# A hybrid attention and mLSTM layer whose input projection is computed by Strassen's seven products

## The chip, the cores and the metric

The kernel runs on one core of a Trainium2 chip. The metric is the device time of one execution in microseconds (us), the median of several runs, lower being better. All arrays are in float32. A float32 product on TensorE is made here from three matmuls in a faster format: each operand is split into a high part (`hi`, the rounded value) and a low part (`lo`, what the rounding left out), and hi·hi, hi·lo and lo·hi are added in PSUM.

## The reference

The layer takes 2048 tokens of width 1024, norms and modulates them, projects them to 4608 columns and 16 gate columns, and sends these into a neighbourhood attention (8 heads of 64, 8 x 16 windows on a grid of 32 x 64 tokens) and a bidirectional mLSTM (4 heads of 128). Both results are gated, joined and projected back to 1024 columns.

```python
h = rmsnorm(h_res, norm_w[l]) * (1.0 + scale[:, None, :]) + shift[:, None, :]
...
proj = h @ w_in + b_in
(na_q, na_k, na_v, na_z, ml_q, ml_k, ml_v, ml_o, ml_z, i_f, f_f, i_b, f_b) = jnp.split(proj, split_idx, axis=-1)
na_out = neighbourhood_attention(na_q, na_k, na_v, rpb) * jax.nn.silu(na_z)
qk = jax.nn.silu(centred_short_conv(jnp.concatenate([ml_q, ml_k], axis=-1), conv_w, conv_b))
...
h_fwd = mlstm_chunkwise(mq, mk, mv, i_f, f_f)
h_bwd = flip(mlstm_chunkwise(flip(mq), flip(mk), flip(mv), flip(i_b), flip(f_b)))
hm = (h_fwd + h_bwd) ... * jax.nn.sigmoid(ml_o)
...
return jnp.concatenate([na_out, ml_out], axis=-1) @ w_out
```

The mLSTM carries, for each head and direction, a 128 x 128 state and a 128-vector through the sequence in chunks (of 128 tokens in this kernel), and each chunk's output needs the state before it. Its queries and keys pass through a convolution over five neighbouring tokens first.

## The kernel before

The tokens lie in SBUF, transposed, as four groups of 512 (`hhi`, `hlo`: 128 partitions x 8 k-tiles x 512). The 4608 columns are 18 blocks of 256; a block's weights are loaded by the SP queue (`load_w`), copied to `hi` by ScalarE (L199, L907) and subtracted to `lo` by GpSimd (L200, L908). The program is one stream per engine, each run in order; a scheduler has fixed that order, and a wait on one instruction holds back all that stands behind it on its engine.

- Start, about 0 to 120 us: modulation vectors on VectorE (L236), row scales, transposes on TensorE (L265), the split into `hi` and `lo` (L270 to L272), and the first two column blocks (L310).
- Token blocks, to about 360 us (`tok_blocks`): six blocks with tokens stationary and 256 columns moving (`mm3`, L513 to L515), results in token rows, evicted by a VectorE addition of the bias (L548, L568), and stored to DRAM. Beside them run the gates' scans and the decay tables (`decays`): GpSimd adds a mask to 128 x 1024 values (L779, 16 times), ScalarE takes eight exponentials of each (L783), and the result goes to the DRAM tile `d_ck`, which holds per head and chunk all that the mLSTM reads.
- Convolution blocks, to about 550 us (`conv_blocks`): four blocks with weights stationary and 512 tokens moving; ScalarE evicts them (L842), VectorE runs the five taps (one L875, four L877), and the queue stores them.
- mLSTM, to about 1005 us (`phase1b`): per head a first pass (`ml_pass1`) that carries the states of both directions over 15 steps and keeps all of them, and a second pass (`ml_pass2`) over 16 chunks that reads a chunk (`ck`), forms scores (L1142), their products (L1155, L1157), the normalised output (L1162 to L1178) and its gate (GpSimd L1179). The last eight blocks' matmuls (`nq_gen`, L934, 512 tokens in the order of the attention's patches) are fed in between by `pump`: 180 ahead, 5.5 a step of pass one and 13 a chunk of pass two.
- Phase 2, to the end: attention over 16 patches, the output projection (L1488) and the last norm. What `pump` has left, up to 108 matmuls, runs in its first slots.

## Time and profile before

| | |
|---|---|
| median of 3 runs | 1398.98 us (1396.51 to 1407.89) |
| the profiled execution's own time | 1400.58 us |
| its span, from first to last instruction | 1398.8 us |
| mean granted TensorE clock | 0.983 |
| TensorE (PE) busy | 1308.0 us, 94% |
| VectorE (DVE) busy | 819.5 us, 59% |
| ScalarE (ACT) busy | 550.2 us, 39% |
| GpSimd (POOL) busy | 261.9 us, 19% |
| moved by DMA | 265.23 MB, mean 190 GB/s |

Busy time counts an instruction from its start to its modelled end, so matmuls that overlap in the pipeline show long durations (0.28 to 0.40 us) although one starts every 0.12 to 0.23 us; the time that a series of them takes is read from start to start. Rows of the profile name a line of the kernel, the engine, the operation, the tile written and the tiles read, shapes, the count, the busy time and the mean in ns, and then how long the engine sat idle before and what ended that idleness.

### The profile page before, as it was taken

What the parts mean: (1) busy time and instruction counts of PE and PEld (TensorE: products, weight loads), DVE (VectorE), ACT (ScalarE), POOL (GpSimd) and SP (SyncE); (2) the same over time, 40 slices, a digit from 0 to 9 for tenths busy, and PEclk for the clock granted to TensorE, in tenths of its full rate; (3) what the DMA queues carried; (4) which work ended last, traced back from release to release, by engine and by line L of the source; (5) the groups of instructions that cost most, each with busy time, mean ns of one, the idle gap of its engine ahead of it and who ended that gap; (6) DMA issues with size and microseconds to landing.
All of it is one profiled execution on the core that took longest, in us unless ns stands there. A gap on an engine that the chain in (4) does not pass through costs nothing. (4 is left out here: it accounts for less than half of the span.)

```text
span 1398.8 us, 23244 instructions
## 1 busy us (share of the span) xinstructions
PE 1308.0 (94%) x8026; PEld 1119.5 (80%) x8026; DVE 819.5 (59%) x2585; ACT 550.2 (39%) x1160; POOL 261.9 (19%) x281
## 2 busy tenths in 40 slices
...
GB/s 370 237 301 159 120 170 228 175 173 195 99 90 216 176 200 161 148 170 158 201 201 218 238 204 249 211 132 174 167 251 227 185 228 169 197 192 170 191 159 75
DMA packets 270090, 265.23 MB, mean 190 GB/s; under 512 B 32746, under 2 KB 232714, under 8 KB 269974
## 3 DMA queue, kind: packets, MB, share of 16 engines
...
## 5 line engine op out<-in xcount | busy, mean ns | idle before, releaser
L934 PE MATMUL pq<-hlo,whi_a 128*128 128x512 f32 x512 | 210.1, 410 | 0.0
L934 PE MATMUL pq<-hhi,whi_a 128*128 128x512 f32 x512 | 210.0, 410 | 0.0
L934 PE MATMUL pq<-hhi,wlo_a 128*128 128x512 f32 x512 | 209.7, 410 | 0.0
L1415 ACT ACTIVATE pbuf<-pbuf,mn 128x480 f32<-128x480 f32 (+5 forms) x128 | 76.4, 597 | 120.9 <-DVE mn L1414 107.3
L934 PEld LDWEIGHTS pq<-hhi,whi_a 128*128 128x128 f32 x512 | 97.4, 190 | 18.0
L934 PEld LDWEIGHTS pq<-hhi,wlo_a 128*128 128x128 f32 x512 | 97.2, 190 | 18.1
L934 PEld LDWEIGHTS pq<-hlo,whi_a 128*128 128x128 f32 x512 | 97.4, 190 | 17.8
L1488 PE MATMUL y<-hhi,whi_a 128*128 128x512 f32 x256 | 84.8, 400 | 0.4 <-ACT whi_a L1461 0.4
L1488 PE MATMUL y<-hhi,wlo_a 128*128 128x512 f32 x256 | 84.4, 399 | 0.0
L1414 DVE CUSTOM_DVE_ANT_0 pbuf<-pS,tab 128x480 f32<-128x480 f32 (+5 forms) x128 | 65.3, 540 | 31.7 <-PE pS L1409 15.6
L908 POOL TENSOR_TENSOR wlo_a<-rawq,whi_a 128x1024 fp32r<-128x1024 f32 x20 | 48.4, 2419 | 162.5 <-ACT whi_a L907 123.8
L1179 POOL TENSOR_TENSOR hm<-hm,ck 128x128 f32<-128x128 f32 x64 | 26.4, 413 | 265.7 <-DVE hm L1178 219.9
L1160 ACT ACTIVATE num<-px,gtile 128x129 f32<-128x129 f32 x120 | 38.4, 365 | 96.1 <-PE px L1155 76.7
L1087 DVE TENSOR_SCALAR wv<-kv,gtile 128x129 f32<-128x129 f32 x120 | 37.0, 315 | 62.8 <-PE dc L1103 35.2
L783 ACT ACTIVATE dec<-dec,gtile 128x128 f32<-128x128 f32 x128 | 41.5, 391 | 79.1 <-POOL dec L779 76.4
L1451 PE MATMUL pO<-pt,v 128*64 128x128 f32 (+3 forms) x832 | 61.8, 283 | 9.9 <-ACT pt L1438 9.4
L548 DVE TENSOR_TENSOR stv<-pv,brow 128x256 f32<-128x256 f32 x32 | 12.2, 419 | 95.4 <-DMA d_vna<-stv 59.1
L1451 PEld LDWEIGHTS pO<-pt,v 128*64 128x64 f32 (+3 forms) x832 | 45.5, 137 | 26.6 <-issue 11.9
L1436 PE MATMUL pT<-ident,pbuf 128*128 128x128 f32 (+2 forms) x416 | 59.8, 283 | 1.7 <-DVE pbuf L1426 1.7
L1438 ACT ACTIVATE pt<-pT 96x384 f32<-96x384 f32 (+3 forms) x128 | 57.7, 500 | 0.7 <-PE pT L1436 0.7
L779 POOL TENSOR_TENSOR dec<-dec,mask 128x1024 f32<-128x1024 f32 x16 | 38.1, 2381 | 94.2 <-DMA dec<-d_mneg 78.2
L1488 PEld LDWEIGHTS y<-hhi,whi_a 128*128 128x128 f32 x256 | 47.2, 188 | 10.0 <-ACT whi_a L1461 0.6
...
## 6 DMA issues: line engine op xcount, KB each, us to landing
...
kv<-d_ck SPq DMA_DIRECT2D x120, 128.5 KB
...
```

What stands on the lines that cost most here:

```text
L779: nc.gpsimd.tensor_tensor(t, t, mask.unsqueeze(2).broadcast_to([P, 2, 4, CH]), ALU.add)
L783: nc.scalar.activation(t[:, d, o, :], t[:, d, o, :], AF.Exp, bias=self.cols["g"][:, d, h, c : c + 1])
L908: nc.gpsimd.tensor_tensor(lo[:, :, cs], raw, hi[:, :, cs].bitcast(F32), ALU.subtract)
L934: nc.tensor.matmul(patch_ps(ps) if patch else ps, w, self.htok(h, g, k, patch), start=(k == 0 and n == 0), stop=(k == KT - 1 and n == 2))
L1087: nc.vector.tensor_scalar(wv, tiles[d, i][:, 128:257], self.cols["w"][:, d, h, c : c + 1], None, ALU.mult)
L1160: nc.scalar.activation(num[:, d, :], px[:, d, :], AF.Copy, scale=self.cols["inter"][:, d, h, c : c + 1])
L1414: nc.vector.tensor_tensor_reduce(pt[:, :nk], ps, tabs[place[u]][j][:, :nk], 1.0, 3e38, ALU.add, ALU.min, mn)
L1415: nc.scalar.activation(pt[:, :nk], pt[:, :nk], AF.Exp, bias=mn, scale=-1.0, accum_out=sums[:, j : j + 1])
L1436: nc.tensor.transpose(ps[:cs, i, :], pts[j][:, i * cs : (i + 1) * cs], self.ident)
L1438: nc.scalar.activation(t[:cs, :nch, :], ps[:cs, :nch, :], AF.Copy)
L1451: nc.tensor.matmul(po[j * HD : (j + 1) * HD, :], v[:n, h * HD : (h + 1) * HD], pt[j][:n, i, :], start=(i == 0), stop=(i == nch - 1))
L1488: nc.tensor.matmul(y, m[:, k, :], w[k][:, cs], start=(k == 4 and n == 0), stop=(k == 3 and n == 2))
```

## The change

The input projection is a product of a 2048 x 1024 token matrix with a 1024 x 256 weight matrix, 18 times. Tokens are taken in two pairs of groups, (2, 3) first and (0, 1) after it. Within a pair the token matrix is cut into four quarters (two groups by two halves of the 1024), and the weights too (two halves of the 1024 by two of the 256 columns), and seven products of quarters or sums of quarters, with further sums, take the place of eight. `stream` runs them: every product is 12 matmuls of 128 x 512 (four k-tiles, three each), with weights stationary, so 2 x 18 x 7 x 12 = 3024 matmuls in all.

- Token operands: `first` and `second` transpose the tokens, form four sums on VectorE (`sums`) and split eight quarters into `hi` and `lo` (`halved`, on GpSimd and VectorE).
- Weight operands: seven per block, four of them sums (`make_sums`, VectorE), each split by ScalarE and GpSimd (`rounded`; one of seven by VectorE) into a ring of eight tiles. The upper stream makes them and stores each one (0.5 MB) to the DRAM tile `d_w`; the lower stream loads them again (`provide`).
- Results: three copies (ScalarE) and four additions (VectorE) per block put the seven products together (`result`). All blocks now come out with channels on partitions; the six that are wanted in token rows are transposed (`turned`). The patch order is made by the eviction's access pattern. Gate columns are computed apart (`gate_rows`).
- The convolution runs over a pair of groups; the two tokens on the border are repaired at the end (`fix_border`). The zero edges are set by GpSimd instead of VectorE.
- The decays run in the lower stream: GpSimd adds the mask and the gate column (two operations on 128 x 1024 values per group), ScalarE takes one exponential; the loads for it are issued by GpSimd.
- The table fills, the output weights' scaling and the tables' rows run in the upper stream.
- mLSTM: pass one carries the backward state only, with its weighting on GpSimd; pass two carries the forward state along (`forward`), reads whole `d_ck` rows, and the first scaling of its output is on ScalarE. Twelve blocks of the lower stream are fed in between by `pump`: 60 ahead, 3.5 a step and 12 a chunk. All of them are drained before phase 2.
- Phase 2 loads all keys from DRAM at its start; half of them lay in SBUF before.

```diff
-PUMP0 = 180
-PUMP1 = 5.5
-PUMP2 = 13
-PUMP3 = 5
+NB = 18
+UPPER, LOWER = (2, 3), (0, 1)
+DENSE = 6
+PUMP0 = 60
+PUMP1 = 3.5
+PUMP2 = 12
...
-    def mm3(self, ps, lhi, llo, rhi, rlo):
-        nc = self.nc
-        for k in range(KT):
-            nc.tensor.matmul(ps, lhi(k), rhi(k), start=(k == 0), stop=False)
-            nc.tensor.matmul(ps, lhi(k), rlo(k), start=False, stop=False)
-            nc.tensor.matmul(ps, llo(k), rhi(k), start=False, stop=(k == KT - 1))
...
-    def ch_tile(self, ps, slot, sub, g, patch=False):
-        hi, lo = slot
-        self.mm3(
-            ps,
-            lambda k: hi[:, k, sub * P : (sub + 1) * P],
-            lambda k: lo[:, k, sub * P : (sub + 1) * P],
-            lambda k: self.htok(self.hhi, g, k, patch),
-            lambda k: self.htok(self.hlo, g, k, patch),
-        )
...
+        upper = self.stream(0, UPPER, self.upper_hook)
+        self.first(upper)
...
+        lower = self.stream(NB, LOWER, lambda n: None)
+        self.second(lower)
...
+        self.chain = itertools.chain(self.gate_chain(cp, self.gates), self.decays(cp))
+        for at in lower:
+            if at == (DENSE - 1, "p3", 11):
+                break
...
+    def sums(self, f11, f12, f21, f22):
+        nc = self.nc
+        nc.vector.tensor_add(f22, f21, f22)
+        nc.vector.tensor_sub(f21, f11, f21)
+        nc.vector.tensor_sub(f11, f22, f11)
+        nc.vector.tensor_sub(f12, f12, f11)
...
+    def gate_rows(self, pair):
+        nc = self.nc
+        for gi, terms in enumerate(((("a11", 0), ("a12", KH)), (("s1", 0), ("a22", KT)))):
+            ps = self.turn_tile(f"pg_{pair[gi]}")[0:32]
+            for j, (nm, k0) in enumerate(terms):
+                for k in range(KH):
+                    for n, h in enumerate(self.op[nm, k]):
...
+    def rounded(self, q, i, src, eng=None):
+        nc = self.nc
+        t = self.wpart(q, i)
+        nc.scalar.activation(t[:, 0], src, AF.Copy)
+        (eng or nc.gpsimd).tensor_tensor(t[:, 1], src, t[:, 0].bitcast(F32), ALU.subtract)
+        dst = self.d_w[ORDER_UPPER[q], i]
+        store = lambda: nc.sync.dma_start(dst, t.bitcast(F32).rearrange("p h k c -> p (h k c)"))
+        if q < 2:
+            store()
+        else:
...
+    def make_sums(self, q, which=(2, 3, 4, 5)):
+        nc = self.nc
+        b11, b12, b21, b22 = self.quarters(q)
+        if 2 in which:
+            self.t2[q] = t2 = self.sp.tile([P, GT], F32, tag="sp", name=f"t2_{q}").rearrange("p (a b) -> p a b", a=KH)
+            nc.vector.tensor_sub(b11, b12, b11)
+            nc.vector.tensor_sub(t2, b22, b11)
+            nc.vector.tensor_sub(b21, b21, t2)
+            nc.vector.tensor_sub(b12, b22, b12)
+        for i in which:
+            if i == 2:
+                self.rounded(q, i, self.t2.pop(q), nc.vector)
+            else:
+                self.rounded(q, i, {3: b12, 4: b11, 5: b21}[i])
...
+    def provide(self, q, i):
+        if q < NB:
+            if i == 5:
+                self.make_sums(q)
+            elif i in (0, 1, 6):
+                self.make(q, i)
+        elif q < 2 * NB:
+            t = self.wpart(q, i)
+            self.nc.sync.dma_start(t.bitcast(F32).rearrange("p h k c -> p (h k c)"), self.d_w[ORDER_LOWER[q - NB], i])
...
+    PRODUCTS = {
+        "p1": ("x", "a11", "b11", True),
+        "p2": ("w", "a12", "b21", True),
+        "p6": ("x", "s2", "t2", False),
+        "p7": ("y", "s3", "t3", True),
+        "p5": ("x", "s1", "t1", False),
+        "p4": ("v", "a22", "t4", True),
+        "p3": ("x", "s4", "b22", False),
+    }
...
+        for n in range(2, NB):
+            plan += [(n, "p1"), (n - 1, "p4"), (n - 1, "p3"), (n, "p2"), (n, "p6"), (n, "p7"), (n, "p5")]
+        plan += [(NB - 1, "p4"), (NB - 1, "p3")]
+        for n, pn in plan:
+            q, blk = q0 + n, order[n]
...
+            w = self.wpart(q, i)
+            for k in range(KH):
+                hi, lo = self.op[a, k]
+                for m, (wh, h) in enumerate(((0, hi), (0, lo), (1, hi))):
+                    nc.tensor.matmul(ps, w[:, wh, k], h, start=(first and k == 0 and m == 0), stop=(k == KH - 1 and m == 2), skip_group_check=True)
+                    if k < KH - 1 or m < 2:
+                        yield n, pn, 3 * k + m
+            self.result(q, blk, pn, pair)
+            self.provide(*divmod(7 * q + i + 8, 7))
+            self.boundary()
+            yield n, pn, 11
...
+        if pn == "p1":
+            copied(1, 0)
+        elif pn == "p2":
+            placed(0, 0, w, c.pop((q, 1)))
+        elif pn == "p6":
+            copied(2, 0)
+        elif pn == "p7":
+            nc.vector.tensor_add(c[q, 2], y, c[q, 2])
+        elif pn == "p5":
+            copied(3, 1)
+            placed(1, 1, y, c.pop((q, 3)))
+        elif pn == "p4":
+            placed(0, 1, v, c.pop((q, 2)))
+        else:
...
+    def turned(self, blk, s, g, f):
+        ps = self.turn_tile(f"tt_{blk}_{s}_{g}")
+        for j in range(4):
+            nc.tensor.transpose(ps[:, j * P : (j + 1) * P], f[:, j * P : (j + 1) * P], self.ident)
...
+        nc.vector.tensor_copy(a[:, GT + 2 : GT + 4], b[:, 2:4])
+        nc.vector.tensor_copy(b[:, 0:2], a[:, GT : GT + 2])
+        nc.gpsimd.memset(a[:, 0:2], 0.0)
+        if g0 == UPPER[0]:
+            nc.gpsimd.memset(b[:, GT + 2 : GT + 4], 0.0)
...
             nc.gpsimd.tensor_tensor(t, t, mask.unsqueeze(2).broadcast_to([P, 2, 4, CH]), ALU.add)
-            for d in range(2):
-                for o in range(4):
-                    c = 4 * gi + o
-                    nc.scalar.activation(t[:, d, o, :], t[:, d, o, :], AF.Exp, bias=self.cols["g"][:, d, h, c : c + 1])
+            nc.gpsimd.tensor_tensor(t, t, self.cols["g"][:, :, h, cs].unsqueeze(3).broadcast_to([P, 2, 4, CH]), ALU.add)
...
+            nc.scalar.activation(t, t, AF.Exp)
...
-        self.st = [[None] * NC for _ in range(2)]
+        self.st = [None] * NC
...
         def weight(i):
-            for d in range(2):
-                c = i if d == 0 else NC - 1 - i
-                wv = ml.tile([P, 129], F32, tag=f"wv{d}", bufs=2, name=f"wv_{h}_{d}_{i}")
-                nc.vector.tensor_scalar(wv, tiles[d, i][:, 128:257], self.cols["w"][:, d, h, c : c + 1], None, ALU.mult)
-                wvs[d, i] = wv
+            c = NC - 1 - i
+            wvs[i] = ml.tile([P, 129], F32, tag="wv1", bufs=2, name=f"wv_{h}_1_{c}")
+            nc.gpsimd.tensor_scalar(wvs[i], tiles[i][:, 128:257], self.cols["w"][:, 1, h, c : c + 1], None, ALU.mult)
...
+        def weight(c):
+            wvs[c] = ml.tile([P, 129], F32, tag="wv0", bufs=2, name=f"wv_{h}_0_{c}")
+            nc.gpsimd.tensor_scalar(wvs[c], vo[c][0], self.cols["w"][:, 0, h, c : c + 1], None, ALU.mult)
+        def forward(c):
+            dc = self.ms.tile([P, GT], F32, tag="s1", bufs=3, name=f"dc_{h}_0_{c}")[:, :129]
+            nc.tensor.matmul(dc, kt.pop(c), wvs.pop(c), start=True, stop=True)
+            new = ml.tile([P, 129], F32, tag="stf", bufs=2, name=f"stf_{h}_{c}")
+            if c == 0:
+                nc.vector.tensor_copy(new, dc)
+            else:
+                nc.vector.scalar_tensor_tensor(new, fw[c], self.decay[:, h, c : c + 1], dc, ALU.mult, ALU.add)
+            fw[c + 1] = new
...
-            nc.vector.tensor_scalar(t, num[:, 0, 0:128], r[:, 0:1], None, ALU.mult)
+            nc.scalar.activation(t, num[:, 0, 0:128], AF.Copy, scale=r[:, 0:1])
...
+        def keys(ct, cols):
...
+        for ct in range(NH // 2):
+            keys(ct, slice(T // 2, T))
```

Two places of the order of instructions, first GpSimd's while it works on the decay tables. Before, it stands in the token blocks; `stvo` is the staging tile of a token block's results, `wlo` the low part of a weight block, `dec` a decay table.

```order
L779 TENSOR_TENSOR dec_1_2232<-dec_1_2232,mask 128x1024
L560 MEMSET stvo_0_2164 128x4
L200 TENSOR_TENSOR wlo_a<-raw_0_2155,whi_a 128x4x256
L200 TENSOR_TENSOR wlo_a<-raw_1_2159,whi_a 128x4x256
L560 MEMSET stvo_1_2306 128x4
L779 TENSOR_TENSOR dec_2_2334<-dec_2_2334,mask 128x1024
```

Now it stands in the lower stream; `u` is the input tile of the convolution, and L696 sets its edge.

```order
L962 DMA dec_3_4717<-d_mneg 128x512 x2
L971 TENSOR_TENSOR dec_2_4692<-dec_2_4692,mask 128x1024
L696 MEMSET u_1_0_4802 128x2
L696 MEMSET u_0_0_4845 128x2
L972 TENSOR_TENSOR dec_2_4692<-dec_2_4692,gtile 128x1024
L962 DMA dec_0_4741<-d_mneg 128x512 x2
L971 TENSOR_TENSOR dec_3_4717<-dec_3_4717,mask 128x1024
L972 TENSOR_TENSOR dec_3_4717<-dec_3_4717,gtile 128x1024
```

A table takes two operations and two DMA issues of GpSimd instead of one operation, and the small MEMSETs that open a convolution tile are queued among them.

The second place is VectorE in the convolution blocks. Before, the taps follow one another with edge copies and MEMSETs of VectorE's own, and no eviction stands among them.

```order
L847 COPY u_0_1_3871<-u_0_2_3909 128x2
L846 COPY u_0_3_3948<-u_0_2_3909 128x2
L875 TENSOR_SCALAR acc_k_2_3962<-u_0_2_3909,cw 128x512
L877 SCALAR_TENSOR_TENSOR acc_k_1_3914<-u_0_1_3871,cw,acc_k_1_3914 128x512
L877 SCALAR_TENSOR_TENSOR acc_k_2_3962<-u_0_2_3909,cw,acc_k_2_3962 128x512
```

Now, in the lower stream, evictions stand behind taps; `py` and `pv` are PSUM banks, `c` a partial sum, `hal` the kept border tokens.

```order
L714 TENSOR_SCALAR acc_0_5008<-u_0_0_4845,cw 128x512
L716 SCALAR_TENSOR_TENSOR acc_1_4817<-u_1_1_4712,cw,acc_1_4817 128x512
L716 SCALAR_TENSOR_TENSOR acc_0_5008<-u_0_0_4845,cw,acc_0_5008 128x512 x2
L605 TENSOR_TENSOR c_21_4884<-py_4911,c_21_4884 128x512
L595 TENSOR_TENSOR u_1_1_4950<-py_4911,c_21_4948 128x512
L695 COPY u_0_1_5000<-u_0_0_4845 128x2
L701 COPY u_0_1_5000<-hal 128x2
L702 COPY hal<-u_1_1_4950 128x2
L595 TENSOR_TENSOR u_0_1_5000<-pv_4987,c_21_4884 128x512
```

The additions L605 and L595, which free TensorE's banks, are queued behind the first tap (L714) of `u_0_0_4845`, whose edge is set by GpSimd's MEMSET of the piece above.

1216 lines of the change are left out of this document (569 added, 647 removed).

## The prediction

> **What bounds the kernel now.** I read the page's busy times first, then the busy time by stage, then the timeline of TensorE inside each stage, and last what it waited for.
>
> ```profile
> PE 1308.0 (94%) x8026; PEld 1119.5 (80%) x8026; DVE 819.5 (59%) x2585; ACT 550.2 (39%) x1160; POOL 261.9 (19%) x281
> ```
>
> ```profile
> 0.00:60.00 60.00, 33.30 (x199) 30.72 (x200) 42.06 (x79) 29.02 (x45) 35.49 (x33) 0.94 0.80 303
> 60.00:360.00 300.00, 280.36 (x2261) 274.38 (x2261) 83.41 (x229) 139.41 (x253) 64.03 (x44) 0.97 0.72 190
> 360.00:557.00 197.00, 192.70 (x860) 154.91 (x859) 125.53 (x238) 58.78 (x87) 20.84 (x8) 1.00 0.63 160
> 557.00:1005.00 448.00, 432.12 (x2299) 360.33 (x2298) 307.25 (x1193) 132.06 (x276) 70.69 (x85) 1.00 0.66 189
> 1005.00:1399.00 394.00, 369.48 (x2415) 299.13 (x2413) 261.21 (x847) 190.90 (x500) 70.87 (x112) 0.97 0.77 188
> ```
>
> A row gives the stretch, its length, the busy time of TensorE, its weight loads, VectorE, ScalarE and GpSimd, the granted clock, the DMA share and GB/s. TensorE is the bound of every stage after the first 60 us. No other engine is above 70% there, and VectorE is at 64% (125.53 of 197) in the convolution stage.
>
> What TensorE's work costs is the distance from one start to the next:
>
> ```profile
> 271.78 0.28 PE L514 MATMUL pv<-wlo_a,hhi 128*128 128x256 f32 x1
> ...
> 273.91 0.28 PE L514 MATMUL pv<-wlo_a,hhi 128*128 128x256 f32 x1
> ```
>
> ```profile
> 504.63 0.40 PE L514 MATMUL pc<-hlo,whi_a 128*128 128x512 f32 x1
> ...
> 507.87 0.40 PE L513 MATMUL pc<-hhi,whi_b 128*128 128x512 f32 x1
> ```
>
> ```profile
> 739.67 0.39 PE L934 MATMUL pq<-hhi,wlo_a 128*128 128x512 f32 x1
> 739.90 0.40 PE L934 MATMUL pq<-hhi,whi_a 128*128 128x512 f32 x1
> 740.14 0.39 PE L934 MATMUL pq<-hlo,whi_a 128*128 128x512 f32 x1
> 740.37 0.40 PE L934 MATMUL pq<-hhi,wlo_a 128*128 128x512 f32 x1
> ```
>
> The first pair spans 18 starts, 0.118 us each at 256 columns; the second 14, 0.231 us at 512; the last rows 0.233 us at 512 in patch order. Patch order costs nothing worth naming, and a 512-wide matmul costs no more per column than two of 256.
>
> **The projection's matmuls.** Before: 2304 of 256 columns (six blocks), 768 of 512 (convolution), 1536 in patch order. 2304 x 0.118 + 768 x 0.231 + 1536 x 0.233 = 272 + 177 + 358 = 807 us. After: 3024 x 0.231 = 699 us. **Minus 108 us**, all on the engine that bounds.
>
> **What TensorE gets in addition.** Six blocks come out channel-major and are turned back: 48 tiles of four transposes. Four transposes take 0.35 us before the next matmul starts:
>
> ```profile
> 47.44 0.60 PE L265 MATMUL tp<-ident,x 128*128 128x128 f32 x4
> 47.79 0.37 PE L310 MATMUL pvo<-whi_a,hhi 128*128 128x272 f32 x1
> ```
>
> 48 x 0.35 = 17 us. The gate columns are 64 matmuls of 512, 15 us. **Plus 32 us.**
>
> **The start.** Up to 360 us the matmuls of the six blocks (272) and 32 groups of transposes (11) leave 77 us unused. They go to the first 60 us and to stalls such as this one:
>
> ```profile
> DVE stv L548 <- DMA d_vna<-stv: 59.1, 5, 20.4
> ```
>
> ```profile
> 346.11 0.58 PE L513 MATMUL pv<-whi_b,hhi 128*128 128x256 f32 x1 [10.12 <-DVE stv L548]
> 346.49 0.42 PE L514 MATMUL pv<-wlo_b,hhi 128*128 128x256 f32 x1
> 346.71 0.41 PE L515 MATMUL pv<-whi_b,hlo 128*128 128x256 f32 x1
> ...
> 351.61 0.33 PE L514 MATMUL pv<-wlo_b,hhi 128*128 128x256 f32 x1
> 351.78 0.28 PE L515 MATMUL pv<-whi_b,hlo 128*128 128x256 f32 x1
> ```
>
> VectorE waited 20.4 us for a staging tile whose store had not landed, TensorE 10.12 us for VectorE, although the DMA engines were at 0.6 to 0.7. Behind it the matmuls start 0.21 us apart, near twice 0.118.
>
> The new start is a chain of VectorE and GpSimd. These rows carry it:
>
> ```profile
> L236 DVE CUSTOM_DVE_ANT_0 junk<-wmod,crow 128x1024 f32<-128x1024 f32 x16 | 26.9, 1682 | 0.3
> L272 DVE TENSOR_TENSOR hlo<-h,hhi 128x512 fp32r<-128x512 f32 x24 | 16.6, 691 | 39.2 <-ACT hhi L271 39.2
> L908 POOL TENSOR_TENSOR wlo_a<-rawq,whi_a 128x1024 fp32r<-128x1024 f32 x20 | 48.4, 2419 | 162.5 <-ACT whi_a L907 123.8
> ```
>
> Modulation is the same bytes in half pieces, 27 us; 32 operations for the token sums and their low parts and ten for the weight sums are 42 x 0.69 = 29 us; GpSimd's 19 low parts at half of 2.42 us are 23 us. Done one after another, which the rows on the taps below ask for, with some 6 us of small operations that is 85 us, in which TensorE has only 60 matmuls and 32 groups of transposes, 25 us. So 60 us are lost where 77 were: **minus 17 us**. If the two engines overlap fully it is 23 us less. `second` has eight low parts on GpSimd ahead of its first product: **plus 10 us** (0 if it runs under the last blocks of the upper stream).
>
> **mLSTM.** A chunk of pass two is now:
>
> ```profile
> 740.60 0.61 PE L1155 MATMUL px<-st,ck 128*128 128x129 f32 x4
> 741.05 0.61 PE L1157 MATMUL pi<-ck 128*128 128x129 f32 x4
> ...
> 744.74 0.61 PE L1155 MATMUL px<-st,ck 128*128 128x129 f32 x4
> ```
>
> ```profile
> L1113 DVE SCALAR_TENSOR_TENSOR st<-st,gtile,dc 128x129 f32<-128x129 f32 x112 | 35.8, 345 | 0.5 <-PE dc L1103 0.3
> ```
>
> That is 4.14 us, filled with projection matmuls. One state product moves from a step of pass one into the chunk, one fill goes: about 4.1 us as before. VectorE gains the state update (0.345 us, L1113) and loses a scaling to ScalarE; GpSimd's weighting replaces VectorE's. TensorE stays in front, so I price this part at nothing beyond the products already counted. The cover is TensorE's own fill; without it a chunk costs VectorE's chain.
>
> **The boundary.** The 108 matmuls that filled phase 2's first slots (25 us) are among the 108 us saved, but a slot without fill waits for its own softmax, and the first keys (4 MB, at the 408 GB/s below 10 us) come after everything is drained. **Plus 10 us**, between 0 (loads run under the last chunk) and 25.
>
> TensorE alone then gives 1400.6 - 108 + 32 - 17 + 10 + 10 = 1328 us. The profiled execution is 1.6 us over the median, so **1326 us** for the median.
>
> **What VectorE and GpSimd take from each other.**
>
> ```profile
> 429.24 0.74 DVE L877 SCALAR_TENSOR_TENSOR acc_k<-u,cw,acc_k 128x512 f32<-128x512 f32 x1
> ...
> 429.90 0.48 DVE L875 TENSOR_SCALAR acc_k<-u,cw 128x512 f32<-128x512 f32 x1
> 430.29 3.54 DVE L877 SCALAR_TENSOR_TENSOR acc_k<-u,cw,acc_k 128x512 f32<-128x512 f32 x2
> 430.86 5.26 POOL L200 TENSOR_TENSOR wlo_a<-raw,whi_a 128x1024 fp32r<-128x1024 f32 x2 [66.04 <-DMA d_t<-d_e]
> 433.76 2.38 DVE L846 COPY u<-u 128x2 f32<-128x2 f32 x1
> ```
>
> Beside GpSimd's two subtractions two taps took 3.54 us instead of 1.48, and a copy of two columns 2.38. An eviction out of PSUM was not held: 0.42 us in the middle of a mask.
>
> ```profile
> 262.25 2.39 POOL L779 TENSOR_TENSOR dec<-dec,mask 128x1024 f32<-128x1024 f32 x1 [5.84 <-DMA d_t<-d_e]
> ```
>
> ```profile
> 262.99 0.42 DVE L548 TENSOR_TENSOR stv<-pv,brow 128x256 f32<-128x256 f32 x1 [2.42 <-PE pv L515]
> ```
>
> So the times of GpSimd's operations and of VectorE's with two operands in SBUF add up. In the four convolution blocks of the upper stream that is, per block, 6 x 1.2 = 7.2 of low parts, 4 x (0.48 + 4 x 0.74) = 13.8 of taps and 5 x 0.69 = 3.5 of weight sums: 24.5 us against 84 x 0.231 = 19.4 of TensorE. Excess 5 us, four times, 20 us; one block of it may trail in the `u` tiles and be caught up later. In the lower stream the decays now take 32 x 2.39 = 76 us of GpSimd instead of 38, and they cannot start before the gates' scan, about two blocks in. 16 tap groups are 55 us. 131 us meet four blocks of TensorE, 78 us: excess 53 us, 14 of them (60 fills) behind the ahead-of-mLSTM pump. The evictions stand behind taps, taps behind GpSimd's MEMSETs, MEMSETs behind decays: TensorE waits. Lower end 0, if the operations fall into gaps; upper end 20 + 53 = 73. I take 10 + 30 = **40 us**, near the middle, since the cover of half the lower excess is visible and the rest is not. Forecast: **1366 us**.
>
> **DMA.** The upper stream moves d_w 66 MB, weights 19, modulation and tokens 17, fills 12.5, output and gate weights 12.6, results 24, table rows 7: 158 MB.
>
> ```profile
> DMA packets 3365, 12.25 MB, mean 408 GB/s; under 512 B 374, under 2 KB 374, under 8 KB 3365
> ```
>
> ```profile
> DMA packets 21438, 17.32 MB, mean 289 GB/s; under 512 B 297, under 2 KB 20783, under 8 KB 21434
> ```
>
> These are the queues from 10 to 40 us and from 60 to 120. At 408 GB/s the 158 MB take 387 us, at 289 they take 547. TensorE's upper stream is 85 + 1452 x 0.231 + 15 = 435 us. The packets of d_w (4 KB) are like the first row's, and I add nothing. [...]
>
> **The rivals.** The one wait of TensorE on GpSimd that is worth a row now:
>
> ```profile
> PE pvo L310 <- POOL hlo L272: 6.6, 3, 2.9
> ```
>
> 1. *TensorE remains the only bound*: **1326 us**. For it: that row has 6.6 us in all. Against it: the rows on taps. 2. *Full exclusion*: the 73 us are paid, and each stall is followed by slow matmuls: from 346.11 to 351.61 us 25 starts, 0.22 us apart where 0.118 is usual, 2.5 us lost; four or five such stalls make 11 us. 1326 + 73 + 11 = **1410 us**. [...] The trace's slow stretch was 5.5 us. 3. *The queue bounds the upper stream*, slower than before: stores of d_w hold ring tiles, and the next weights wait behind them on SP. It decides once the mix moves less than 158 MB in 435 us, 363 GB/s. At 289 the stage takes 547: 1326 + 112 = **1438 us**. For it: the 20.4 us wait for a store at 0.7 load, and the 60 to 120 us row. Against: those packets were under 2 KB. That the seven products are not what runs is excluded: the order has 3024 of them.
>
> **How the numbers follow.** Forecast 1366 (spread 1345 to 1392) 0.40; rival 1 (1312 to 1340) 0.24; rival 2 (1392 to 1428) 0.16; rival 3 (1425 to 1460) 0.20. A measurement of this kernel can tell about 1% from no change, so faster is below 1385, slower above 1413. Faster: 0.24 + 0.34 of the forecast's 0.40 = 0.58. Same: 0.06 + 0.10 of rival 2 = 0.16. Slower: 0.06 + 0.20 = 0.26. The range 1312 to 1435 leaves out what may lie under rival 1 (0.08) and half of rival 3 (0.10).
>
> **What would show it.** Matmul rows of L570 starting 0.231 us apart show the saving; PE busy near 1308 - 108 + 32 = 1232 us. Waits of TensorE on VectorE evictions L595 and L605 in the convolution blocks, with taps of 2 to 3 us beside L971 and L972, show the forecast; the same in long stalls, rival 2; weights late with DMA named as releaser and a DMA share near 1 over the upper stream, rival 3. A first product stream that is steady before 70 us, or a lower stream of 135 us, would prove me too slow; a chunk of pass two above 4.5 us would prove the mLSTM's price of nothing wrong.

## The result, and the profile after

The changed kernel takes 1693.58 us (median of 4 runs, 1691.83 to 1695.42) where the kernel before takes 1401.01 beside it: 1.208 times as long, 95% interval 1.203 to 1.214. The forecast was 1366, and the range ended at 1435. The profiled execution has a span of 1693.2 us.

The page's busy times and its total of moved bytes:

```profile
PE 1343.7 (79%) x6821; PEld 1054.9 (62%) x6821; DVE 915.4 (54%) x2546; ACT 678.4 (40%) x1369; POOL 455.3 (27%) x545
...
DMA packets 286554, 393.78 MB, mean 233 GB/s; under 512 B 37458, under 2 KB 210842, under 8 KB 286438
```

TensorE has 1205 instructions fewer than before and is busy 36 us longer, in a span longer by 294. TensorE's and VectorE's shares of the span fall, ScalarE's rises by one per cent and GpSimd's from 19 to 27, so no engine has become the bound over the whole. 129 MB more are moved. By stage (stretch, length, busy time of TensorE, weight loads, VectorE, ScalarE, GpSimd, then granted clock, DMA share, GB/s):

```profile
0.00:110.00 110.00, 57.65 (x271) 43.99 (x272) 73.25 (x184) 52.59 (x99) 38.74 (x39) 0.86 0.79 261
110.00:271.00 161.00, 151.04 (x667) 118.82 (x666) 111.15 (x171) 73.72 (x115) 57.95 (x56) 0.98 0.90 286
271.00:616.00 345.00, 247.62 (x915) 182.59 (x915) 105.56 (x158) 112.39 (x181) 82.25 (x63) 0.83 0.75 258
616.00:870.00 254.00, 186.37 (x779) 141.22 (x779) 135.07 (x232) 111.76 (x147) 106.77 (x97) 0.86 0.69 208
...
870.00:1250.00 380.00, 344.21 (x1860) 283.00 (x1859) 224.05 (x913) 134.76 (x315) 98.99 (x178) 0.96 0.80 258
...
1250.00:1361.00 111.00, 38.80 (x200) 29.38 (x199) 40.02 (x141) 30.29 (x70) 14.25 (x25) 0.63 0.88 215
1361.00:1693.00 332.00, 318.00 (x2139) 255.88 (x2137) 226.31 (x748) 162.85 (x445) 56.32 (x88) 0.98 0.69 167
```

TensorE is at 94% from 110 to 271 us and at 96% in the last stretch. In between it is at 72%, 73%, 91% and 35%. I cut at the blocks of the stream, counting L570 matmuls in the timeline by 84 (good to some 3 us): the first eight blocks end at 271 us, the lower stream's first block (block 18 of 36) starts at 616, block 25 at 870, and the products end at 1250. The prediction's sum for TensorE alone, 1328 us, splits the same way. The upper stream's 435 stands in it. Phase 2 is 394 - 25 + 10 = 379. The mLSTM is 448 us of before without the matmuls that now lie elsewhere (1428 then, 924 from block 25 on; 504 x 0.233 = 117), so 331. The rest, 183, is the lower stream to block 25.

| stage | the sum | measured | over the sum |
|---|---|---|---|
| start and upper stream | 435 | 616 | 181 |
| lower stream, to block 25 | 183 | 254 | 71 |
| mLSTM, to the last product | 331 | 380 | 49 |
| phase 2 | 379 | 443 | 64 |

The forecast had put 40 on top, 10 in the first row and 30 in the second. The loss is in every stage, so one cause can't be all of it. The list of waits has the longest of TensorE, and one of ScalarE that stands behind the first of them:

```profile
PE px L570 <- ACT ring L477: 46.6, 10, 11.6
...
PE pS L1442 <- DVE mn L1448: 43.5, 2, 32.6
...
PE px L570 <- ACT c L587: 37.4, 13, 15.5
...
PE tp L275 <- DVE diag L365: 32.4, 2, 21.9
...
ACT ring L477 <- DMA d_w<-ring: 28.5, 15, 9.3
...
PE tp L273 <- ACT f L277: 25.6, 8, 14.7
```

Four of these five have a stage of their own: weights in the upper stream (L477), phase 2's first scores (L1442), the lower convolution blocks (L587), the passage between the streams (L273); L275 is the start. The first, followed back through three engines' timelines, begins on SP:

```profile
386.02 0.34 SPq L993 DMA_DIRECT2D wraw<-in_w_out_dram  x1
386.46 1.12 SPq L1001 DMA_DIRECT2D d_wo<-wraw  x1
387.63 5.22 SPq L811 DMA_DIRECT2D d_e<-d_rneg  x8
392.90 2.97 SPq L480 DMA_DIRECT2D d_w<-ring  x4
```

```profile
395.68 0.63 ACT L477 ACTIVATE ring<-raw 128x512 fp32r<-128x512 f32 x1 [5.31 <-DMA d_w<-ring]
```

```profile
387.62 0.39 PE L570 MATMUL px<-1_s,ring 128*128 128x512 f32 x1
...
389.25 0.40 PE L570 MATMUL px<-0_s,ring 128*128 128x512 f32 x1
397.79 0.79 PE L570 MATMUL px<-0_s,ring 128*128 128x512 f32 x1 [8.14 <-ACT ring L477]
...
402.51 0.40 PE L570 MATMUL px<-1_s,ring 128*128 128x512 f32 x1
402.75 0.39 PE L570 MATMUL px<-0_s,ring 128*128 128x512 f32 x1
```

Eight issues of table columns (L811, 0.65 us each) stand on SP ahead of four stores of d_w. No store was issued from 372 to 392.9 us. ScalarE waits 5.31 us for a ring tile whose store is late, TensorE 8.14 us for ScalarE. The ten matmuls that follow take 4.7 us instead of 2.3.

### The profile page after: what moved, and what is told of

Same layout as the page of the kernel before. It is cut to its first block, busy times and chain, and to the rows that moved or that the text cites. A ratio compares the mean times of both kernels' runs of the same rounds, so it can differ in the third digit from the quotient of the medians.

```text
span 1693.2 us, 21978 instructions
## 1 busy us (share of the span) xinstructions
PE 1343.7 (79%) x6821; PEld 1054.9 (62%) x6821; DVE 915.4 (54%) x2546; ACT 678.4 (40%) x1369; POOL 455.3 (27%) x545
## 4 chain that ended last, share of the span: by engine, by line
PE 39%; DMA 26%; DVE 11%; POOL 8%; issue 7%; SPq 6%; ACT 3%; ACTq 0%; POOLq 0%; DVEq 0%
PE y L1522 10%; PE px L570 8%; DMA ck<-d_ck 5%; DMA dec<-d_mneg 3%; PE pv L570 3%; PE pO L1485 3%; PE pT L1470 3%; DVE acc L716 3%; PE py L570 2%; DMA kv<-d_ck 2%; DMA d_wo<-wraw 2%; POOL ring L478 2%; SPq L833 2%; POOL dec L971 2%; DMA d_mix<-zt 2%
## 5 line engine op out<-in xcount | busy, mean ns | idle before, releaser
L570 PE MATMUL px<-0_s,ring 128*128 128x512 f32 x864 | 321.4, 429 | 77.3 <-ACT c L587 37.4
L570 PEld LDWEIGHTS px<-0_s,ring 128*128 128x128 f32 x864 | 173.0, 202 | 129.2 <-ACT c L587 45.5
L478 POOL TENSOR_TENSOR ring<-raw,ring 128x512 fp32r<-128x512 f32 x108 | 146.6, 1370 | 371.7 <-ACT ring L477 314.9
L570 PE MATMUL px<-1_s,ring 128*128 128x512 f32 x432 | 183.8, 425 | 0.8 <-DVE 1_s L295 0.8
L1522 PE MATMUL y<-wohi,mix 128*128 128x512 f32 x512 | 172.5, 410 | 6.6 <-ACT mix L1495 4.4
L587 ACT ACTIVATE c<-px,bcol 128x512 f32<-128x512 f32 x108 | 73.5, 682 | 156.2 <-PE px L570 143.6
L570 PE MATMUL pw<-0_a,ring 128*128 128x512 f32 x288 | 106.8, 424 | 12.5 <-DVE o L595 10.4
L570 PE MATMUL px<-0_a,ring 128*128 128x512 f32 x288 | 104.5, 417 | 14.7 <-ACT ring L477 13.7
L570 PE MATMUL py<-0_s,ring 128*128 128x512 f32 x288 | 106.0, 424 | 11.0 <-DVE u L595 8.0
L716 DVE SCALAR_TENSOR_TENSOR acc<-u,cw,acc 128x512 f32<-128x512 f32 x128 | 113.7, 922 | 0.6
L570 PE MATMUL pv<-0_a,ring 128*128 128x512 f32 x288 | 109.6, 438 | 5.5 <-DVE o L595 5.3
L477 ACT ACTIVATE ring<-raw 128x512 fp32r<-128x512 f32 x108 | 65.7, 626 | 91.0 <-DMA d_w<-ring 28.5
L570 PEld LDWEIGHTS px<-1_s,ring 128*128 128x128 f32 x432 | 87.6, 203 | 17.8 <-DVE 1_s L295 1.2
L1442 PE MATMUL pS<-kk,qhigh 128*128 128x480 f32 (+5 forms) x128 | 43.9, 347 | 53.2 <-DVE mn L1448 43.5
L570 PEld LDWEIGHTS px<-0_a,ring 128*128 128x128 f32 x288 | 56.1, 196 | 29.8 <-ACT ring L477 14.8
L570 PEld LDWEIGHTS py<-0_s,ring 128*128 128x128 f32 x288 | 57.6, 201 | 26.5 <-DVE u L595 9.3
L570 PEld LDWEIGHTS pw<-0_a,ring 128*128 128x128 f32 x288 | 56.8, 198 | 27.1 <-DVE o L595 13.2
```

The source lines that it names most:

```text
L477: nc.scalar.activation(t[:, 0], src, AF.Copy)
L478: (eng or nc.gpsimd).tensor_tensor(t[:, 1], src, t[:, 0].bitcast(F32), ALU.subtract)
L570: nc.tensor.matmul(ps, w[:, wh, k], h, start=(first and k == 0 and m == 0), stop=(k == KH - 1 and m == 2), skip_group_check=True)
L587: nc.scalar.activation(c[q, i], x, AF.Identity, bias=bias[s])
L716: nc.vector.scalar_tensor_tensor(acc, src, w, acc, ALU.mult, ALU.add)
L1442: nc.tensor.matmul(o, qhigh[at][:, j, c, :], kv, start=True, stop=False)
```

## The experiments

Starts of blocks, in us, counted in the same way (the scheduler sets the upper stream's last product now ahead of the passage to the lower stream, now behind it, so the start of block 18 compares to some 5 us); block 18 opens the lower stream, blocks 20 to 22 are three of its convolution blocks (58 us at 84 x 0.231 each), from block 25 on the mLSTM runs:

| kernel | median | block 18 starts | blocks 20 to 22 take | block 25 starts |
|---|---|---|---|---|
| changed | 1693.6 | 616 | 137 | 870 |
| d_w stored by ScalarE's queue | 1661.0 | 585 | 140 | 852 |
| half of d_w | 1662.5 | 571 | 142 | 842 |
| 1/8 of d_w | 1596.6 | 552 | 132 | 803 |
| no tables, no scaled output weights | 1593.4 | 521 | 138 | 776 |
| no tables | 1608.1 | 534 | 138 | 789 |
| tables issued by GpSimd | 1643.6 | 557 | 142 | 828 |
| decays as before | 1693.7 | 609 | 139 | 866 |
| exponentials a group later | 1692.6 | 618 | 142 | 878 |
| no decay additions | 1660.8 | 619 | 109 | 844 |
| no exponentials | 1673.2 | 620 | 104 | 858 |
| one tap of five | 1672.9 | 610 | 126 | 853 |
| edges set by VectorE | 1684.6 | 619 | 138 | 872 |
| tokens not loaded again | 1684.6 | 616 | 136 | 862 |
| all of the dear things left out | 1487.1 | 480 | 88 | 694 |
| four re-orderings | 1663.0 | 571 | 142 | 841 |

### The upper stream: stores of d_w, or what stands among them

```diff
-        store = lambda: nc.sync.dma_start(dst, t.bitcast(F32).rearrange("p h k c -> p (h k c)"))
+        store = lambda: nc.scalar.dma_start(dst, t.bitcast(F32).rearrange("p h k c -> p (h k c)"))
```

> Only the queue that issues the 126 stores of weight operands is changed, from SP to ScalarE's. Queue theory: in the upper stream (0 to 610 us of the changed kernel) the stores stand on SP behind the table columns, table rows and the scaling of the output weights, ring tiles stay occupied, and TensorE waits for weights; then the upper stream falls from 610 to 470-530 us and the kernel from 1694 to 1560-1620 us. Bandwidth theory: the same 158 MB move, so 1670-1700 us. VectorE-GpSimd theory of the prediction: nothing about that changes, 1680-1700 us.

1661.01 us, ratio 1.182 (1.173 to 1.191): 33 us back, all of them ahead of block 18, and less than the queue theory asked for, more than the bandwidth theory. Blocks 8 to 16 still take 24 to 40 us each.

```diff
-        store = lambda: nc.sync.dma_start(dst, t.bitcast(F32).rearrange("p h k c -> p (h k c)"))
+        store = lambda: nc.sync.dma_start(dst[:, :GT], t.bitcast(F32)[:, 0].rearrange("p k c -> p (k c)"))
...
+            self.nc.sync.dma_start(t.bitcast(F32).rearrange("p h k c -> p h (k c)"), self.d_w[ORDER_LOWER[q - NB], i][:, :GT].unsqueeze(1).broadcast_to([P, 2, GT]))
```

> Only the high half of each weight operand is stored (33 MB fewer bytes written in the upper stream; same count and order of transfers); the lower stream loads that half twice, 0.5 MB as before, so its low parts are not the right ones. Bandwidth theory: 125 instead of 158 MB, the upper stream falls from 610 to about 490 us, kernel about 1570 us. Queue theory: the stores still stand behind the same transfers; they land a little sooner, 1640-1690 us.

1662.46 us, ratio 1.183 (1.174 to 1.192), 31 us back. That is the queue theory's range; the bandwidth theory had 1570.

```diff
-        store = lambda: nc.sync.dma_start(dst, t.bitcast(F32).rearrange("p h k c -> p (h k c)"))
+        store = lambda: nc.sync.dma_start(dst[:, :P], t.bitcast(F32)[:, 0, 0])
...
+            self.nc.sync.dma_start(t.bitcast(F32)[:, 0, 0], self.d_w[ORDER_LOWER[q - NB], i][:, :P])
```

> Each store and each reload of a weight operand keeps its place and its waits but moves 64 KB instead of 512, so 132 MB become 16 (the lower stream works with the wrong weights). Bandwidth theory: upper stream 610 to 480-510 us, lower stream and mLSTM 40-60 us less, kernel 1500-1540 us. Side work and queue order: 1600-1650 us, about twice the 31 us that half of the bytes of one direction brought.

1596.58 us, ratio 1.137 (1.125 to 1.149), just below the range of queue order and far above that of bandwidth. Some 65 us come back ahead of block 18 and 35 in the mLSTM, which reloads weights all along (the stretch from block 25 to the last product):

```profile
805.00:1150.00 345.00, 330.00 (x1862) 275.75 (x1861) 226.99 (x921) 136.22 (x316) 100.44 (x180) 1.00 0.62 187
```

345 us at a clock of 1.00, against 380 at 0.96 for the changed kernel. So of the mLSTM's 49 us over the sum 35 are the reloads.

```diff
-            self.tables_columns(n - CONV_END - 2)
-                self.tables_rows(m // 3, m % 3)
...
-            nc.vector.tensor_tensor(raw, raw, gate[:, cs], ALU.mult)
-            nc.sync.dma_start(self.d_wo[k][:, cs], raw)
+            nc.sync.dma_start(self.d_wo[k], self.w_out[:, k, :])
```

> Left out of the upper stream: the 48 small transfers of the table columns, the 72 of the table rows, and the scaling of the output weights by the gate, which becomes eight DRAM-to-DRAM copies without a wait (attention bias and gate are therefore not the right ones). Stores and reloads of the weight operands stay as they are. Theory that this side work holds up the weights (its transfers stand on SP and its multiplications on VectorE ahead of stores and evictions): blocks 8 to 16 of the upper stream fall from 26-41 us each to 21-24, 90 to 120 us in all, kernel 1575-1605 us. Bandwidth theory: some 8 MB of 158 less, 10-25 us, 1670-1685 us.

1593.41 us, ratio 1.135 (1.126 to 1.143), as the first theory had it. Blocks 10 to 16 fall to 20 to 25 us, with the 66 MB of d_w still stored.

```diff
-            self.tables_columns(n - CONV_END - 2)
-                self.tables_rows(m // 3, m % 3)
```

> The changed kernel without the tables' columns and rows in the upper stream (about 50 small DMAs of SP; the tables stay unfilled, so the attention's bias is missing). The scaling of the output weights stays. Run without both, the upper stream was 95 us shorter. If the small DMAs that stand between the weight stores on SP's queue made most of it, the lower stream starts at about 545 us instead of 616 and the median is near 1620. If the output weights' 32 transfers did, the start is near 595 and the median near 1670.

1608.12 us, ratio 1.147 (1.143 to 1.150): the tables' columns and rows alone are 82 of the 95 us. What the DMA engines did in the stretch of the columns (48 transfers of 7.5 KB), first in the changed kernel (271 to 420 us), then without tables (271 to 414), in 40 slices of busy tenths and GB/s, and in all:

```profile
DMA  9978894341329999797363399999856519899989
GB/s 309 372 235 244 292 277 118 109 129 72 80 61 409 264 363 365 252 324 229 113 195 73 112 405 289 341 333 321 254 146 152 145 23 404 253 323 390 309 276 387
DMA packets 26476, 36.31 MB, mean 244 GB/s; under 512 B 7666, under 2 KB 16882, under 8 KB 26470
```

```profile
DMA  9969695405998999997799999999889999999999
GB/s 330 360 175 328 172 350 166 150 2 193 320 368 213 366 366 274 319 294 292 303 314 288 339 324 349 326 333 368 291 228 387 379 403 337 329 387 396 396 380 383
DMA packets 24269, 43.89 MB, mean 307 GB/s; under 512 B 1771, under 2 KB 12916, under 8 KB 24261
```

Without some 5900 packets of under 512 B, 7.6 MB more pass in 6 us less. SP issued the 48 transfers in three runs of 16, at 298 to 314, 340 to 355 and 376 to 393 us. In the second and third the rate falls to 73 to 195 and to 23 to 152 GB/s, where without tables it is 288 to 339 and 228 to 403. In those slices the DMA engines are busy for 3 to 6 tenths, and once for 1: the small packets don't fill them. The low slices of the first run prove less, since there is a hole of 2 to 193 GB/s at 292 to 307 us without tables too.

```diff
-            nc.sync.dma_start(self.d_e[ct][:, i, :, start - k0 : start - k0 + 16], self.d_rneg[:, :, dx : dx + 16])
+            nc.gpsimd.dma_start(self.d_e[ct][:, i, :, start - k0 : start - k0 + 16], self.d_rneg[:, :, dx : dx + 16])
...
-            nc.sync.dma_start(
+            nc.gpsimd.dma_start(
                 t[:, r * 16 : (r + 1) * 16, j0 : j0 + 8 * nk],
```

> The changed kernel with the 120 DMAs of the tables' columns and rows issued by GpSimd instead of SP; the result is the same. If they cost by their place in SP's order (weight stores and loads stand behind them), the lower stream starts at 545 to 575 us instead of 616 and the median is below 1660. If they cost by what their small packets take of the DMA engines, or GpSimd's issuing takes as much from the low parts, the start stays between 600 and 630 and the median at 1680 to 1705.

1643.62 us, ratio 1.172 (1.168 to 1.176). The same 120 DMAs, issued by GpSimd, and block 18 starts 60 us earlier, as the first expectation had it; from block 8 to 541 us, 3 us short of the last product ahead of the passage, the row is

```profile
272.00:541.00 269.00, 223.15 (x893) 166.67 (x892) 102.54 (x144) 99.89 (x162) 145.17 (x176) 0.94 0.94 320
```

320 GB/s where the changed kernel moves 258. So what the tables cost, 82 us when they are left out, is above all their place in SP's order. At the start of block 25 some 42 of the 60 us are left: block 18 takes 60 us instead of 51, and the next ones a little longer too; what they wait for I didn't separate.

### The lower convolution blocks

The timelines of GpSimd, ScalarE, VectorE and TensorE at one place of the changed kernel:

```profile
736.64 2.33 POOL L971 TENSOR_TENSOR dec<-dec,mask 128x1024 f32<-128x1024 f32 x1 [5.59 <-DMA dec<-d_mneg]
738.92 0.13 POOL L696 MEMSET u<- 128x2 f32 x2
739.05 1.89 POOL L972 TENSOR_TENSOR dec<-dec,gtile 128x1024 f32<-128x1024 f32 x1
```

```profile
740.98 1.06 ACT L976 ACTIVATE dec<-dec 128x1024 f32<-128x1024 f32 x1 [9.41 <-POOL dec L972]
742.05 1.28 ACT L717 ACT_TABLE_LOAD   x1
...
743.35 0.72 ACT L717 ACTIVATE acc<-acc,cb 128x512 f32<-128x512 f32 x1
```

```profile
739.05 2.18 DVE L714 TENSOR_SCALAR acc<-u,cw 128x512 f32<-128x512 f32 x1 [6.97 <-POOL u L696]
741.15 6.91 DVE L716 SCALAR_TENSOR_TENSOR acc<-u,cw,acc 128x512 f32<-128x512 f32 x4
```

```profile
744.13 1.11 PE L727 MATMUL kt<-ident,acc 128*128 128x128 f32 x4 [9.87 <-ACT acc L717]
```

Four taps take 6.91 us instead of four times 0.74, the first one 2.18 instead of 0.48, which is the exclusion that the forecast rests on. The rows show two more things. GpSimd's MEMSET stands behind an addition that waited 5.59 us for a load, and VectorE 6.97 us behind the MEMSET. And ScalarE, in order, stands 9.41 us at an exponential that waits for GpSimd, with the Silu behind it for which TensorE waits 9.87 us.

```diff
-            nc.gpsimd.tensor_tensor(t, t, self.cols["g"][:, :, h, cs].unsqueeze(3).broadcast_to([P, 2, 4, CH]), ALU.add)
...
-            nc.scalar.activation(t, t, AF.Exp)
+                    nc.scalar.activation(t[:, d, o, :], t[:, d, o, :], AF.Exp, bias=self.cols["g"][:, d, h, c : c + 1])
```

> The decays are formed as in the kernel before: one addition on GpSimd (16 instead of 32 of 2.37 us) and eight exponentials with a bias on ScalarE. In the lower stream (620 to 870 us) ScalarE stood 54 us in front of an exponential that GpSimd had not readied, with the PSUM copies for TensorE queued behind it. Theory that the decays on GpSimd hold up that stage: 35-60 us less, 1635-1660 us. Rival, the reloads of the weights bound that stage: no change, 1685-1700 us. Second rival, ScalarE's 38 us of extra exponentials take the place: 1680-1720 us.

1693.72 us, ratio 1.205 (1.196 to 1.215), nothing, as the two rivals had it. GpSimd has 30 us less to do, ScalarE 112 exponentials more. The waits say why half of the additions is worth so little, first in the changed kernel, then here:

```profile
POOL dec L971 <- DMA dec<-d_mneg: 43.6, 11, 6.0
```

```profile
POOL dec L971 <- DMA dec<-d_mneg: 69.9, 15, 6.4
ACT dec L978 <- POOL dec L971: 59.0, 13, 7.0
```

GpSimd's additions wait for the loads of their tables, 26 us longer than before, and ScalarE waits for GpSimd as long as before (59.0 us, 54.3 in the changed kernel). In both kernels the 16 tables take some 125 us from the first exponential to the last, 8 us each. A load is issued behind an addition and lands a median of 5.7 us later, so the loads are a rival to the additions as the pace of the decays; no run here leaves them out.

```diff
-            nc.scalar.activation(t, t, AF.Exp)
+            late.append((t, h, cs))
+            if len(late) > 1:
+                finish(*late.pop(0))
```

> Each exponential of the decays is issued one group later, so that ScalarE does not stand in front of it while GpSimd still adds; its operations are the same. Theory that ScalarE's 54 us of standing there, with PSUM copies queued behind, costs the lower stream: blocks 20 to 22 of it fall from 136 to about 100 us, kernel 1650-1665 us. Rival, VectorE's taps and GpSimd's additions exclude each other, whatever ScalarE does: under 15 us, 1680-1700 us.

1692.56 us, ratio 1.205 (1.195 to 1.216), nothing. ScalarE still waits 58 us for the additions: a group later they aren't done either.

```diff
+            if n == 0:
                 nc.gpsimd.tensor_tensor(t, t, mask.unsqueeze(2).broadcast_to([P, 2, 4, CH]), ALU.add)
...
```

> The changed kernel with GpSimd's two additions on the decay tables done for the first of 16 groups only (the decays are wrong; loads, exponentials and stores stay). If GpSimd's 76 us of additions, which hold VectorE's taps and stand ahead of the MEMSETs of the convolution, are what the lower convolution blocks 20 to 22 wait for, these three blocks take 60 to 75 us instead of 136, and the median falls by 60 or more to about 1630. If it is something else (taps and evictions queued in order on VectorE, reloads of weights, the broadcast loads on the DMA queues), they still take over 120 and the median stays above 1670.

1660.77 us, ratio 1.184 (1.180 to 1.188). Blocks 20 to 22 take 109 us, 28 less, between the two expectations; from block 19 to 25 it is 173 us against 203. TensorE still waits 31.4 us there for ScalarE's copies (L587), and the exponentials now wait for loads.

```diff
-            nc.scalar.activation(t, t, AF.Exp)
-                nc.scalar.dma_start(dst, t[:, d])
+                nc.gpsimd.dma_start(dst, t[:, d])
```

> The changed kernel without the exponentials of the decay tables (the decays are wrong); GpSimd's additions stay, and the tables are stored by GpSimd's queue, so nothing on ScalarE waits for GpSimd there. Without the additions (the run before) blocks 20 to 22 took 108 us instead of 136. If ScalarE's queue is the larger part, since the copies of product banks (L587) stand behind exponentials that wait for GpSimd or for a load, the three blocks take 75 to 95 us and the median is near 1640. If GpSimd's time beside VectorE's taps is what counts, they take over 120 and the median is above 1670.

1673.24 us, ratio 1.191 (1.186 to 1.197). With the additions there and nothing of the decays on ScalarE the three blocks take 104 us, 33 less, though GpSimd issues the stores too; the next block takes 41 instead of 23, and 20 us remain at the end. This is between the two expectations again. TensorE no longer waits for ScalarE's copies L587 in these blocks (31.7 us in the changed kernel), but up to the end of the next block 43.9 us for the convolution's Silu (L717), which waits for VectorE's taps. So in these blocks what stands on ScalarE is worth as much as GpSimd's time, over the whole less (20 us against 33). That the 28 and the 33 us are mostly the same ones, since the exponentials wait for GpSimd, is likely and not shown; no run has both and nothing else gone.

```diff
-        for j in range(5):
+        for j in range(5 if g in UPPER else 1):
```

> The changed kernel with one tap instead of five in the lower stream's convolution (its queries and keys are wrong there). It takes 16 x 4 taps, about 47 us, off VectorE. If evictions queued behind taps hold TensorE in blocks 20 to 22, they take 80 to 95 us instead of 136 and the median is about 1645. If GpSimd's operations or the DMAs bound them, they stay above 120 and the median above 1675.

1672.88 us, ratio 1.191 (1.184 to 1.199): 11 us in the three blocks, 21 in all, from 57 us of VectorE (104.6 busy from block 19 to 25, then 48).

```diff
-        nc.gpsimd.memset(a[:, 0:2], 0.0)
+        nc.vector.memset(a[:, 0:2], 0.0)
```

> The changed kernel with the convolution's edge MEMSETs (L696) on VectorE, as before the change; the result is the same. On GpSimd each stands behind the decays' additions and behind their DMA issues, which wait, and taps and evictions stand behind it. If that queue place is what is left in the lower convolution blocks, blocks 20 to 22 take 95 to 115 us instead of 136 and the median is about 1665. If the exclusion between GpSimd's and VectorE's operations and ScalarE's queue are all of it, they stay above 125 and the median above 1680.

1684.56 us, ratio 1.204 (1.200 to 1.208). The three blocks take 138 us: the MEMSET's place in GpSimd's queue, which the timeline makes look dear, costs nothing there. It is one of several that are late together.

```diff
-                    self.load_x(4 * LOWER[1] + 2 * i + j, raw[:, j * D : (j + 1) * D])
+                    self.xt[4 * LOWER[1] + 2 * i + j] = self.xt[4 * LOWER[0] + 2 * i + j]
```

> The changed kernel with the second half of the lower tokens not loaded: the first half's tiles are used again (the lower half of the output is wrong). Four loads of 0.5 MB that wait for the last weight tiles, and sit at the start of the second stream, are gone. If the passage from the upper to the lower stream is bound by these loads, blocks 17 and 18 take 50 to 60 us instead of 100 and the median is about 1650. If it is bound by the chain of transposes, splits and sums on ScalarE, VectorE and GpSimd, they take 90 to 100 and the median stays above 1680.

1684.62 us, ratio 1.202 (1.196 to 1.207). Blocks 17 and 18 take 89 us instead of 100. The passage is not bound by these loads.

### The mLSTM and phase 2

The kernel before with the change's two passes of the mLSTM, and nothing else:

```diff
-            for d in range(2):
-                c = i if d == 0 else NC - 1 - i
+            c = NC - 1 - i
...
+            nc.gpsimd.tensor_scalar(wvs[c], vo[c][:, 0:129], self.cols["w"][:, 0, h, c : c + 1], None, ALU.mult)
...
+                nc.vector.scalar_tensor_tensor(new, fw[c], self.decay[:, h, c : c + 1], dc, ALU.mult, ALU.add)
...
-            nc.vector.tensor_scalar(t, num[:, 0, 0:128], r[:, 0:1], None, ALU.mult)
+            nc.scalar.activation(t, num[:, 0, 0:128], AF.Copy, scale=r[:, 0:1])
```

> The kernel before with the mLSTM part of the change alone (pass one backward only, forward state carried in pass two, weighting on GpSimd, first output scaling on ScalarE). Prediction's price of nothing: 1390-1410 us. Rival, the longer chain through a chunk of pass two costs 0.3-0.5 us per chunk: 1415-1435 us. Rival, one chunk load fewer and less work on VectorE gain: 1370-1385 us.

1413.54 us (10 runs) against 1402.66 (13 runs), ratio 1.0074 (1.0046 to 1.0102): a loss of 11 us, where the prediction priced nothing.

The last two rows of the changed kernel's stages above are cut at the 25th of phase 2's 256 score matmuls. The like stretches of before, from the end of the mLSTM on:

```profile
1005.00:1066.00 61.00, 50.56 (x260) 40.42 (x259) 25.73 (x63) 24.47 (x51) 11.51 (x19) 0.92 0.94 255
1066.00:1399.00 333.00, 318.92 (x2157) 258.71 (x2155) 235.48 (x785) 166.43 (x450) 59.36 (x93) 0.99 0.74 175
```

The long part is the same, 332 us and 333. The head is 111 us instead of 61, with TensorE idle for 72 of them and the DMA engines at 0.88; TensorE waits 32.6 us there for the first results of VectorE, and those for their tables:

```profile
DVE pbuf L1448 <- DMA tab<-d_t: 43.4, 4, 21.8
```

```diff
-            nc.sync.dma_start(wolo[k].bitcast(F32), self.d_wo[k])
+            nc.gpsimd.dma_start(wolo[k].bitcast(F32), self.d_wo[k])
...
-            keys(ct, slice(0, T // 2))
+            keys(ct, slice(0, T // 2), nc.gpsimd)
```

> At the head of phase 2 the output weights and the second half of the keys are issued by GpSimd's queue instead of SP's; the bias tables no longer stand behind 24 transfers. Theory that TensorE's 33 us wait at 1337 us is for a table in that queue: 25-40 us less, 1655-1670 us. Rival, the DMA engines (0.91 busy there) are the limit: no change, 1685-1700 us.

1690.46 us, ratio 1.204 (1.195 to 1.212), no change.

```diff
-        for ct in range(NH // 2):
-            keys(ct, slice(T // 2, T))
+        keys(0, slice(T // 2, T))
...
+        for ct in range(1, NH // 2):
+            keys(ct, slice(T // 2, T))
```

> The changed kernel with phase 2's loads in another order: of the keys' second half only the first unit's 1 MB stands ahead of the first queries and tables, the other 3 MB behind them; the result is the same. If the first scores wait for the order of the loads, they start some 15 us earlier and the median falls by 12 to 25 to about 1675. If the whole 8 MB of keys and the output weights bound the head of phase 2 by the DMA engines' time, the waits move to the next units and the median stays at 1688 to 1698.

1686.85 us, ratio 1.203 (1.198 to 1.207). The first score starts at 1269 instead of 1283, and the 25th at 1353 instead of 1361. From its products' end the head is 108 us:

```profile
1245.00:1353.00 108.00, 36.00 (x171) 26.98 (x172) 36.30 (x125) 27.42 (x63) 13.22 (x23) 0.61 0.88 216
```

Queue and order are worth 3 and 7 us. The changed kernel's transfers from 1262 to 1345 us, with the DMA engines at 0.91 of that stretch:

```profile
DMA packets 9977, 17.81 MB, mean 215 GB/s; under 512 B 2136, under 2 KB 6520, under 8 KB 9974
```

That the head lasts as long as its transfers fits this share and is argued: no run took bytes out of it.

### The sum of it

All of these at once: no tables, no scaled output weights, 1/8 of d_w, no decay additions but one, no exponentials, one lower tap of five, tokens not loaded again.

> The changed kernel with everything left out that the runs so far showed to be dear, at once: table columns and rows, the output weights' scaling, 7/8 of the storing and loading of d_w, the decays' additions and exponentials, four of five lower taps, and the second load of lower tokens. The products, the start, the convolution's evictions, the mLSTM and phase 2 stay. If these causes account for the loss, the lower stream starts at 470 to 490 us, its six dense blocks take 140 to 160 us, and the median is near 1440; what is then left over 1326, by the sum made for TensorE alone, is the start, the passage between the streams, the mLSTM and phase 2. If clock and banks hold the products anyway, blocks stay at 25 us or more and the median is above 1520.

1487.09 us, ratio 1.060 (1.057 to 1.062): still slower than the kernel before, which does all that work. By stage, from block 8 on:

```profile
264.00:480.00 216.00, 209.53 (x906) 165.46 (x904) 86.22 (x140) 102.30 (x170) 73.99 (x56) 0.98 0.48 147
480.00:694.00 214.00, 178.61 (x805) 136.86 (x805) 64.58 (x170) 82.40 (x126) 75.83 (x109) 0.92 0.51 147
694.00:1047.00 353.00, 333.68 (x1866) 278.80 (x1865) 227.25 (x920) 137.64 (x318) 97.06 (x175) 0.99 0.59 179
1047.00:1487.00 440.00, 355.80 (x2317) 283.92 (x2315) 263.18 (x879) 192.07 (x511) 69.65 (x111) 0.89 0.74 180
```

Now TensorE is at 97% of the upper stream. The upper stream ends as expected (470 to 490), but the six dense blocks (18 to 23) take 195 us and not 140 to 160, and the median is 47 over the expected 1440. Against the sum for TensorE alone 45, 31, 22 and 61 us remain in the four stages. The single gains of the parts, 100 + 97 + 33 + 20 + 21 + 9 = 280 us, give 206 together.

Last, what order alone can get back, with the same result: d_w stored by ScalarE's queue, tables issued by GpSimd, phase 2's loads re-ordered, edges set by VectorE.

> The changed kernel with four re-orderings at once, the result being the same: d_w stored by ScalarE's queue (alone 33 us), table columns and rows issued by GpSimd (alone 50), the loads of phase 2 in the other order (alone 7), and the edge MEMSETs on VectorE. If the gains add, the lower stream starts near 525 us and the median is 1590 to 1605. If the first two remove the same wait, it starts near 541 as with GpSimd's queue alone, and the median is 1620 to 1640. Either way it stays over 1404: the work that was moved on to the DMA engines and the small engines is still there.

1662.95 us, ratio 1.187 (1.185 to 1.190), which is 19 us worse than the tables on GpSimd alone, outside both expectations. Block 18 starts at 571 us, against 557 with the tables on GpSimd alone (the expectation puts that at 541). With d_w's stores on it, ScalarE's queue has them among its evictions: in the upper stream VectorE waits 26.3 us for ScalarE's copies (L587), against 15.9 us with the tables moved alone. That this is what costs the 19 us is argued, not shown.

## Why the prediction was wrong

*The saving is there.* Matmuls of L570 start 0.233 us apart where nothing is late (389.25 less 387.62 is 1.63 for seven), and with the dear work gone ten blocks of the upper stream take 216 us, where the price with transposes is 197. **The step "minus 108 us" was right for TensorE, and its condition, that TensorE stays the bound, was not.** "PE busy near 1232" came out at 1343.7. 60 us of that go with slow clock: the run with the dear work left out has the same 6821 instructions in 1283.6, at a mean granted clock of 0.945 instead of 0.898. The other 52 I didn't follow up.

*"DMA ... I add nothing" is the step that failed most.* The bytes were right, 158 MB estimated, the rate was not; the trace up to 616 us has

```profile
DMA packets 115639, 163.71 MB, mean 266 GB/s; under 512 B 13185, under 2 KB 79553, under 8 KB 115608
```

which is below even the 289 GB/s of the low end. Rival 3 named the place, stores of d_w that hold ring tiles with weights behind them on SP, and its point of decision, 363 GB/s; its price of 112 us stands against 181. What it lacked is the third party. The table rows were counted as 7 MB and the output weights within 12.6, and not as 120 and 32 issues in SP's order; tables out are worth 82 us, the scaled weights 13 more, storing d_w some 41 more (from 521 to 480, the other parts of that run lying behind it or at its very end), and 45 remain. The order in which they are taken out sets these shares: d_w at 1/8 alone gave 65.

*"The start: minus 17 us".* The first stream is steady at 110 us, not at 85. With 84 products and the gate columns done by then, 24 x 0.231 + 7 = 13 of the 25 us are work that the sum has elsewhere; the start was some 12 us too cheap. TensorE waits 32.4 us there for VectorE's `diag` (L365).

*"Plus 40" for the exclusion.* The exclusion itself is in the rows: four taps took 6.91 us, where four times 0.74 is 2.96. As the step that makes TensorE wait it was wrong. The excess was the sum of GpSimd's additions and VectorE's taps, 131 us, over 78 of TensorE; with half of the additions gone nothing came back, with four of five taps gone 11 us in blocks 20 to 22. These blocks lose 79 us, not 30. That nearly all additions gone are worth 28, close to the 30, is luck, since that run also takes away what the exponentials wait for. The step left out that the exponentials, now waiting for GpSimd, and the evictions share one in-order engine: the diff puts an instruction that waits ahead of copies that free a bank, and I named VectorE's queue for that and not ScalarE's. The sign I gave, waits on the additions L595 in the convolution blocks, is 6.9 us in blocks 20 to 22 and 3.1 in the upper ones, against 31.7 for ScalarE's L587 in blocks 20 to 22, and those 31.7 are gone with the exponentials. 30 us of the 79 remain with additions, exponentials and four taps gone. In the upper convolution blocks 10 stand against some 19 (blocks 1 to 7 take 162 us, 136 by the price, 7 of the rest transposes); how much of that is exclusion was not tried.

*"`second`: plus 10".* Blocks 17 and 18 take 100 us instead of 39, of which 18 are transposes and gate columns; some 40 us, where 10 were priced. Sharing token tiles gives 11 of them back. The rest, a chain of copies, splits and sums on ScalarE, VectorE and GpSimd, was seen in the waits and not tried.

*"mLSTM: nothing".* Its own sign of error came true: the distance from chunk to chunk is 4.56 and 4.97 us:

```profile
1016.16 0.38 PE L1188 MATMUL px<-stf,ck 128*128 128x129 f32 x2
...
1020.72 0.38 PE L1188 MATMUL px<-stf,ck 128*128 128x129 f32 x2
...
1025.69 0.38 PE L1188 MATMUL px<-stf,ck 128*128 128x129 f32 x2
```

11 us of the stage's 49 are the new passes themselves, 35 the reloads of d_w beside them, which the sum had not set against that stage at all (258 GB/s there, 189 before).

*"The boundary: plus 10, between 0 and 25".* The head of phase 2 takes 50 us more than before although 25 us of matmuls have left it. I set 4 MB at 408 GB/s; the head moves 17.8 MB at 215.

*The rivals.* TensorE alone (1326) and full exclusion (1410) are excluded by the stage table: neither has a loss in phase 2 or in the mLSTM. Rival 3 was right in kind for the upper stream and said nothing of the other three, where 184 us lie.

**What stays open:** 31 us of the lower stream, some 20 of them in `second`, that are there with all dear work out; why four re-orderings give less than one; whether the loads of the decay tables or GpSimd's additions set the pace of the exponentials; what the upper stream's remaining 45 us are beyond the 12 of the start; how much of every loss is the slow clock behind a stall and how much the stall.
